# Expert 6's store in five parts on three DMA queues instead of three parts on two

## The chip, the cores and the metric

The kernel runs on one core of one Trainium2 chip. The metric is the device time of one execution in microseconds; a run is one such measurement, and the median of the runs counts. The profile is of one further execution: its span goes from the first to the last instruction that the hardware profiler recorded.

## The reference

Eight experts, each a layer of two products with biases and a ReLU between them, in fp32:

```python
n_experts, capacity, hidden, expert_hidden = 8, 256, 512, 2048
h = np.matmul(x, w1) + b1[:, np.newaxis, :]     # x (8,256,512), w1 (8,512,2048)
h = np.maximum(h, 0)
return (np.matmul(h, w2) + b2[:, np.newaxis, :]).astype(np.float32)   # w2 (8,2048,512)
```

w1 and w2 are 4 MB per expert each, so some 64 MB of weights are read, 4 MB of x, and 4 MB of results are written.

## The kernel before, in words

The experts are e = 0 to 7. All weights come from HBM as fp32 and are cast to fp16 on the way, by DMAs that GpSimd issues (`load_w1`, L84; `load_w2`, L93). Each weight tile is 128 partitions wide, and there are three tiles for w1 and three for w2, so a load waits until TensorE has finished with the tile's earlier contents. w2 of experts 6 and 7 comes in two halves (`HALVED`). x of experts 0 and 1 comes as fp32 through SyncE (L190) and is cast on VectorE; the other x come through GpSimd.

VectorE transposes x in blocks of 32x32 (`transposes`, L109 and L112). `first_product` (L121) makes 16 blocks of h, transposed, of 128x256 each, in PSUM; ScalarE adds the bias and applies ReLU (L128). `second_product` starts both halves of the 256 rows with b2 (a product with ones, L171) and adds the 16 blocks of h times w2 (L178). It runs LAG = 3 experts behind the first product. The GpSimd DMAs stand in an order that is written out by hand in `ring`, and `ordered` keeps program order for them and for the matmuls.

`store` copies the two PSUM halves to SBUF, one on VectorE (L156) and one on ScalarE (L157). The results of experts 0 to 3 and of 4 and 5 are gathered in two tiles (`GROUPS`), which `flush` writes through GpSimd's ring (L140): 2048 KB and 1024 KB, late in the program. The results of experts 6 and 7 are written by `store` itself as soon as the copies are done (L164). Each is a tile of 128 rows, one per partition, with 4 KB a row (two output rows of 512 fp32), 512 KB in all. Expert 7's tile goes out as one DMA by SyncE. Expert 6's is cut into parts by the table `PARTS`, whose entries are first row, row after the last, and whether ScalarE issues it:

```python
PARTS = {E - 2: ((0, 25, False), (25, 121, True), (121, 128, False))}
```

A DMA that SyncE or ScalarE issues goes through a hardware queue (q1 and q10 in the profile); one that GpSimd issues goes through a ring in memory (q0), in which its transfers follow each other.

The order at the end of the program is: GpSimd issues the last halves of w2, then the flush of experts 0 to 3, then that of 4 and 5. SyncE issues the first and third part of expert 6, then expert 7. ScalarE copies half of expert 6, issues its part, and copies half of expert 7. Then SyncE waits for all landings (L261).

Of the kernel before, what the change touches and what calls it, by code (L numbers as in the profile page):

```python
# [10 lines left out]
def kernel(  # L11
# [9 lines left out]
    nc = tc.nc  # L21
    fp32 = mybir.dt.float32
    fp16 = mybir.dt.float16
    E, T, H = x.shape
    M = w1.shape[2]
    P = 128
# [10 lines left out]
    HALVED = (E - 2, E - 1)  # L37


    PARTS = {E - 2: ((0, 25, False), (25, 121, True), (121, 128, False))}  # L40
    nXF32 = 2
    X_LOADS = {2: 2, 4: 4}

    def ordered(ins):
        return tc.keep_in_program_order(ins)
# [96 lines left out]
    def store(e, po):  # L142
        if e in group_of:
            first, n = group_of[e]
            split, rows = n, P // n
            if e == first:
                results[e] = group_pool.tile(
                    [P, split * nTB, H], fp32, tag=f"out{e}", name=f"out{e}")
        else:
            first, n, split, rows = e, 1, 1, P  # L150
            results[e] = out_pool.tile([P, nTB, H], fp32, tag="out", name="out")
        out_sb = results[first]
        at = (e - first) * rows
        for k in range(split):
            part = slice(k * rows, (k + 1) * rows)
            nc.vector.tensor_copy(out=out_sb[at : at + rows, k * nTB, :], in_=po[0][part])  # L156
            nc.scalar.copy(out=out_sb[at : at + rows, k * nTB + 1, :], in_=po[1][part])  # L157
        dst = out[first : first + n].rearrange("e (p r) h -> (e p) r h", r=split * nTB)
        if e in group_of:
            if e == first + n - 1:  # L160
                pending[first] = (dst, out_sb)
            return
        for p0, p1, scalar in PARTS.get(e, ((0, P, False),)):
            (nc.scalar if scalar else nc.sync).dma_start(out=dst[p0:p1], in_=out_sb[p0:p1])  # L164

    def second_product(e):
        po = []
        for tb in range(nTB):
            t = psum_o.tile([P, H], fp32, tag=f"po{tb}", name=f"po{tb}")
            po.append(t)  # L170
            ordered(nc.tensor.matmul(  # L171
                out=t, lhsT=ones1, rhs=b2_sb[0:1, e * H : (e + 1) * H], start=True, stop=False,
            ))
        half = nJ // 2 if e in HALVED else nJ
        for lo in range(0, nJ, half):
            for tb in range(nTB):
                for j in range(lo, lo + half):
                    ordered(nc.tensor.matmul(  # L178
                        out=po[tb],
                        lhsT=hT[e][:, j, tb * P : (tb + 1) * P],  # L180
                        rhs=w2_sb[e][:, j, :],
                        start=False,
                        stop=(j == nJ - 1),
                    ))
        store(e, po)

    x32 = []
    for e in range(nXF32):
# [4 lines left out]
        out=b2_sb,  # L193
        in_=b2.rearrange("e h -> (e h)").rearrange("(o f) -> o f", o=1),
# [12 lines left out]
    for b in range(nB):  # L207
        nc.vector.transpose(  # L208
            out=b1T[b * B : (b + 1) * B, nB - 1 - b : nB - 1 - b + nJ * B],
            in_=b1_rows.rearrange("r (i j) -> r j i", j=nJ),  # L210
# [55 lines left out]
```

## Time and profile before

| | us |
|---|---|
| median of 3 runs | 181.59 |
| lowest and highest run | 181.46, 181.81 |
| span of the profiled execution | 179.7 |
| median of the runs less that span | 1.9 |
| TensorE matmuls busy | 129.1 (72%) |
| VectorE busy | 88.0 (49%) |
| ScalarE busy | 70.2 (39%) |
| GpSimd busy | 13.1 (7%) |
| GpSimd's ring, packets, as a share of 16 DMA engines | 96.6% |
| last issue of a store (expert 7, by SyncE), from the span's start | 173.9 |
| from that issue to its landing | 4.8 |

The profiled execution has no time of its own beside the span. The runs are longer than the span by 1.9 us; the difference lies before the first and after the last recorded instruction.

How to read it: a core has 16 DMA engines, and the page gives their mean busy share in 40 slices. Packets are listed by queue, not by engine. Numbers of DMA landings are from issue to the last of a transfer's data. Times within the span are counted from its start.

### The profile page before, as it was taken

The page shows a single profiled execution, that of the slowest core. Times are in us where ns is not written, and L with a number is a line of the kernel's source. Part 1 is how long each engine was busy: PE and PEld are TensorE (multiplying, and loading weights), DVE is VectorE, ACT ScalarE, POOL GpSimd, SP SyncE. Part 2 cuts the span into 40 slices and gives each one's busy share as a digit, 9 for nine tenths or more (in the row PEclk, how much of TensorE's full clock was granted, in tenths as well). Part 3 has the DMA queues.
Part 4 walks back from the last instruction along what each step waited for, and adds up shares of the span by engine and source line. Part 5 has one row for each costly group of instructions (what it writes and reads, how often), then busy time and mean ns, then how long its engine had stood idle before and what let it go on. Part 6 is the DMA issues. An engine that isn't in the chain of part 4 may idle for free.

```text
span 179.7 us, 1958 instructions
## 1 busy us (share of the span) xinstructions
PE 129.1 (72%) x784; PEld 85.8 (48%) x784; DVE 88.0 (49%) x125; ACT 70.2 (39%) x151; POOL 13.1 (7%) x28
## 2 busy tenths in 40 slices
PE   0005099969595970899969597969497887999950
PEld 0004079969592320795369244844195332433420
DVE  0999942987000199999999998003200020301010
ACT  0000459969593022483099005950586020020010
POOL 7000002120201010001010001000200021010000
PEclk9999999999998798589999889999999996999996
DMA  5999999999999999999999999999999999999996
GB/s 216 251 226 199 233 212 197 233 224 193 228 230 192 221 233 215 197 230 230 204 208 230 219 193 233 226 193 222 230 215 197 233 206 204 223 212 215 335 420 250
DMA packets 3829, 40.56 MB, mean 226 GB/s; under 512 B 461, under 2 KB 477, under 8 KB 1133
## 3 DMA queue, kind: packets, MB, share of 16 engines
q0 software_dynamic: 3232, 38.35, 96.6%
q1 hardware_dynamic: 476, 1.70, 2.4%
q10 hardware_dynamic: 112, 0.39, 0.5%
q8 instruction: 6, 0.10, 0.2%
q14 instruction: 3, 0.02, 0.0%
HBM read 71.39 MB, written 4.19 MB: 421 GB/s over the span
## 4 chain that ended last, share of the span: by engine, by line
DMA 66%; PE 26%; POOL 2%; another core or an unknown queue 1%; issue 1%; ACT 0%; POOLq 0%
DMA w1sb<-in_w_dram 44%; DMA w2sb<-in_w_dram 22%; PE po L178 18%; PE ph L121 8%; PE po L171 1%; POOL w1sb L84 1%; ACT out L157 0%; POOL x L76 0%; POOL b_sb L192 0%; POOL b_rows L196 0%; POOLq L250 0%
## 5 line engine op out<-in xcount | busy, mean ns | idle before, releaser
L121 PE MATMUL ph<-xT,w1sb 128*128 128x256 f16 x512 | 63.6, 289 | 34.8 <-DMA w1sb<-in_w_dram 23.9
L121 PEld LDWEIGHTS <-w1sb 128*128 128x128 f16 x512 | 59.0, 147 | 40.3 <-DMA w1sb<-in_w_dram 32.6
L178 PE MATMUL po<-w2sb,hT 128*128 128x512 f16 x256 | 61.4, 402 | 9.4 <-DMA w2sb<-in_w_dram 9.4
L112 DVE STREAM_TRANSPOSE xT<-x 32x256 f16<-32x256 f16 (+1 forms) x64 | 53.1, 889 | 25.6 <-DMA x<-in_x_dram 18.7
L128 ACT ACTIVATE hT<-ph,b1T 128x256 f16<-128x256 f32 x128 | 56.2, 474 | 13.6 <-PE ph L121 13.4
L178 PEld LDWEIGHTS <-hT 128*128 128x128 f16 x256 | 25.9, 102 | 44.7 <-issue 19.3
L156 DVE COPY out<-po 32x512 f32<-32x512 f32 (+2 forms) x22 | 15.1, 688 | 54.0 <-PE po L178 53.8
L157 ACT COPY out<-po 32x512 f32<-32x512 f32 (+2 forms) x22 | 12.7, 579 | 69.7 <-PE po L178 69.5
L109 DVE STREAM_TRANSPOSE xT<-x 32x256 f16<-32x256 f16 x32 | 14.0, 436 | 0.5
L93 POOL DMA_DIRECT2D w2sb<-in_w_dram x10 | 5.3, 534 | 72.8 <-PE po L178 72.8
L128 ACT ACT_TABLE_LOAD x1 | 1.3, 1283 | 20.5 <-DVE b1T L208 20.5
L84 POOL DMA_DIRECT2D w1sb<-in_w_dram x8 | 4.5, 558 | 63.2 <-PE ph L121 62.4
L171 PE MATMUL po<-b_sb,ones 1*128 1x512 f16 x16 | 4.8, 379 | 0.0
L208 DVE STREAM_TRANSPOSE b1T<-b_rows 32x512 f32<-32x512 f32 x4 | 4.1, 1035 | 0.1
L201 DVE CAST x<-x 128x1024 f16<-128x1024 f32 x2 | 1.5, 757 | 3.3 <-DMA x<-in_x_dram 3.3
L140 POOL DMA_DIRECT2D out_dram<-out x2 | 1.1, 542 | 10.9 <-ACT out L157 10.9
L171 PEld LDWEIGHTS <-ones 1*128 1x128 f16 x16 | 0.9, 92 | 2.1 <-issue 2.1
L76 POOL DMA_DIRECT2D x<-in_x_dram x2 | 1.1, 552 | 0.0
L197 DVE MEMSET ones<- 1x128 f16 x1 | 0.2, 165 | 0.8 <-PEq L250 0.8
L196 POOL DMA_DIRECT2D b_rows<-in_b_dram x1 | 0.5, 515 | 0.0
L192 POOL DMA_DIRECT2D b_sb<-in_b_dram x1 | 0.5, 513 | 0.0
L250 POOL MEMSET const-float32-0.0<- 128x1 f32 x1 | 0.1, 99 | 0.2 <-issue 0.2
(3 smaller groups left out, 0.3 us busy)
## 6 DMA issues: line engine op xcount, KB each, us to landing
w1sb<-in_w_dram POOLq DMA_DIRECT2D x8, 2048.0 KB, 34.5
w2sb<-in_w_dram POOLq DMA_DIRECT2D x6, 2048.0 KB, 46.8
w2sb<-in_w_dram POOLq DMA_DIRECT2D x4, 1024.0 KB, 24.0
out_dram<-out POOLq DMA_DIRECT2D x1, 2048.0 KB, 26.8
x<-in_x_dram SPq DMA_DIRECT2D x2, 512.0 KB, 3.9
x<-in_x_dram POOLq DMA_DIRECT2D x1, 1024.0 KB, 30.8
out_dram<-out POOLq DMA_DIRECT2D x1, 1024.0 KB, 17.8
x<-in_x_dram POOLq DMA_DIRECT2D x1, 512.0 KB, 24.0
```

The source lines that it names most:

```text
L84: ordered(nc.gpsimd.dma_start(out=w1_sb[e], in_=w1[e].rearrange("(p kc) m -> p kc m", kc=nKC)))
L93: ordered(nc.gpsimd.dma_start(out=w2_sb[e][:, lo : lo + half], in_=src[:, lo : lo + half]))
L109: nc.vector.transpose(out=out[:, :, g, :, 0, :], in_=block[:, :, :, 0, :])
L112: nc.vector.transpose(out=out[:, tb, g], in_=block[:, tb])
L121: ordered(nc.tensor.matmul(out=ph, lhsT=w1_sb[e][:, kc, :].rearrange("p (q j) -> p q j", j=nJ)[:, :, j], rhs=xT[e][:, kc, :], start=(kc == 0),
L128: nc.scalar.activation(out=hT[e][:, j, :].rearrange("p (tb k i) -> p tb k i", tb=nTB, k=split), in_=ph.rearrange("p (tb i k) -> p tb k i", ...
L156: nc.vector.tensor_copy(out=out_sb[at : at + rows, k * nTB, :], in_=po[0][part])
L157: nc.scalar.copy(out=out_sb[at : at + rows, k * nTB + 1, :], in_=po[1][part])
L171: ordered(nc.tensor.matmul(out=t, lhsT=ones1, rhs=b2_sb[0:1, e * H : (e + 1) * H], start=True, stop=False,))
L178: ordered(nc.tensor.matmul(out=po[tb], lhsT=hT[e][:, j, tb * P : (tb + 1) * P], rhs=w2_sb[e][:, j, :], start=False, stop=(j == nJ - 1),))
L201: nc.vector.tensor_copy(out=t, in_=x32[e])
L208: nc.vector.transpose(out=b1T[b * B : (b + 1) * B, nB - 1 - b : nB - 1 - b + nJ * B], in_=b1_rows.rearrange("r (i j) -> r j i", j=nJ),)
```

## The change

Expert 6's 128 rows are stored in five parts. ScalarE issues 64 rows (it issued 96). SyncE issues 25 rows as before, though others, and 3 (it issued 7). GpSimd issues 11 and 25 rows into its ring, behind the two flushes, in descriptors of 2 KB, so two for each row. The sum is 128 rows as before. Nothing else in the program is different: the instructions of TensorE, VectorE and ScalarE stand in the same order, and GpSimd has two DMA instructions more, at its end.

```diff
-    PARTS = {E - 2: ((0, 25, False), (25, 121, True), (121, 128, False))}
+    PARTS = {E - 2: (
+        (0, 64, nc.scalar), (64, 89, nc.sync), (89, 100, nc.gpsimd),
+        (100, 125, nc.gpsimd), (125, 128, nc.sync),
+    )}
...
-        for p0, p1, scalar in PARTS.get(e, ((0, P, False),)):
-            (nc.scalar if scalar else nc.sync).dma_start(out=dst[p0:p1], in_=out_sb[p0:p1])
+        for p0, p1, queue in PARTS.get(e, ((0, P, nc.sync),)):
+            if queue is nc.gpsimd:
+                ordered(queue.dma_start(out=dst[p0:p1], in_=out_sb[p0:p1], max_dma_last_dim=2048))
+            else:
+                queue.dma_start(out=dst[p0:p1], in_=out_sb[p0:p1])
```

## The prediction, made before the changed kernel was run

> **What bounds the kernel now.** I began with the page: the slices, then the DMA queues.
>
> ```profile
> span 179.7 us, 1958 instructions
> DMA  5999999999999999999999999999999999999996
> GB/s 216 251 226 199 233 212 197 233 224 193 228 230 192 221 233 215 197 230 230 204 208 230 219 193 233 226 193 222 230 215 197 233 206 204 223 212 215 335 420 250
> ...
> q0 software_dynamic: 3232, 38.35, 96.6%
> q1 hardware_dynamic: 476, 1.70, 2.4%
> q10 hardware_dynamic: 112, 0.39, 0.5%
> q8 instruction: 6, 0.10, 0.2%
> ```
>
> The DMA engines are full in every slice but the first and the last. No compute engine is: PE has 72%. q0 is GpSimd's ring, q1 SyncE's queue, q10 ScalarE's. The six q8 packets are loads of instructions, and they matter below. Next the tail, in windows (core 0; PE, PEld, DVE, ACT, POOL, clock, DMA share, GB/s), and who waits at the end on SyncE.
>
> ```profile
> 166.40:173.90 7.50, 6.89 (x32) 2.94 (x30) 0.69 (x1) 0.57 (x1) 0.00 (x0) 1.00 0.99 377
> 173.90:177.00 3.10, 0.00 (x0) 0.00 (x0) 0.00 (x0) 0.02 (x1) 0.00 (x0) 0.95 0.97 404
> 177.00:178.50 1.50, 0.00 (x0) 0.00 (x0) 0.00 (x0) 0.00 (x0) 0.00 (x0) 0.50 0.63 257
> 178.50:179.70 1.20, 0.00 (x0) 0.00 (x0) 0.00 (x0) 0.00 (x0) 0.00 (x0) 0.50 0.00 0
> ```
>
> ```profile
> SPq L261 <- DMA out_dram<-out: 4.1, 3, 2.4
> ```
>
> All compute is over at 173.9. What follows is stores alone, at 404 GB/s, and then the share drops to 0.63 for 1.5 us: some of the sixteen engines are done and others are not. That part is the whole subject. The chain of waits ends in PE and a copy and does not show it, because the last stores have no instruction behind them:
>
> ```profile
> 166.28 7.03 PE po L178 x32
> 173.31 0.02 issue
> 173.33 0.59 ACT out L157
> ```
>
> The issues say what is in flight then: the two GpSimd flushes (2048 and 1024 KB, still landing at 175 and 177.5), expert 6's three parts, and expert 7's 512 KB.
>
> ```profile
> out_dram<-out POOLq DMA_DIRECT2D x1, 2048.0 KB, 26.8
> out_dram<-out POOLq DMA_DIRECT2D x1, 1024.0 KB, 17.8
> out_dram<-out SPq DMA_DIRECT2D x1, 512.0 KB, 4.8
> out_dram<-out ACTq DMA_DIRECT2D x1, 384.0 KB, 9.1
> ```
>
> **Sixteen ends.** The trace's DMA records give each packet's start, duration, size and queue, but no engine. From 166 us on each packet begins where one before it ended, so they can be chained into sixteen sequences; that is my own reconstruction. A packet of one 4 KB row lies 0.1555 us before the next. The closing 4-byte record of expert 7's store (8 rows on every engine) ends each sequence. Of expert 6's 128 rows:
> - five engines (group A) carry 12: 5 of SyncE's 25, 1 of its 7, 6 of ScalarE's 96. They end at 178.06, 178.25, 178.26, 178.40 and 178.41.
> - two (B) carry 7: 1 and 6. They end at 178.12 and 178.26.
> - nine carry 6, and fall in two sets: four (C) end at 178.29, 178.30, 178.32 and 178.425, five (D) at 177.04, 177.32, 177.37, 177.43 and 177.54.
>
> SyncE's queue has 60 closing records: 16 for each of its two loads and for expert 7, 5 for the 25 rows and 7 for the 7 rows. So 25 rows went to five engines and 7 rows to seven, the same five among them.
>
> Why B and C are late is shown by the closing records of the GpSimd loads: in sorted order they keep their distances from load to load, except that after each of the six instruction loads (36.5, 53.5, 83.9, 105.7, 134.8 and 159.6 us; 0.89 to 0.97 us each) one more sequence drops back by 1.07 to 1.13 us. Six sequences are hit once each, and they are B and C. The first two hit are the lowest two of the late set, which match B. So the instruction queue steps from one engine to the next, starting at B.
>
> **The change, part by part.** The bytes are unchanged, and so is everything up to 166.4 us. What changes is which engine carries which of the 128 rows.
> - ScalarE, 64 rows instead of 96: four on each engine instead of six. One issue of 0.38 us as before.
> - SyncE, 25 rows as before, five on each of A; 3 instead of 7, one on each of three of A. Issue 0.36 and up to 0.60 us, over by 167.4; expert 7's store behind them is issued at 173.94.
> - GpSimd, 11 and 25 rows: two more issues on POOL of 0.54 us each (the two flush rows: 1.1 us). They wait for the two copies of expert 6, done at 166.37; POOL has been free since 160.3, and behind them stands only the end of the program. The second also waits for the eighth-last earlier GpSimd transfer, a w2 load landed at 149.5: no wait. Both are over at about 167.6, and the ring still has flush data until 175.8 to 177.2, so this is hidden; it would cost its 1.1 us only if the ring ran dry.
> - Two transfers more on GpSimd's ring add two closing records on each engine. After a flush such a record takes 6 ns: 0.012 us.
> - Two descriptors of 2 KB for a row: the nearest row is the bias load, whose 4 KB packets (two rows of 2 KB) took 172 ns against 159 for one row. So 0 to 0.013 us a row. It could also be a gain if two were moved together better, which no row suggests.
> - SyncE waits for two more landings at the end. Its waits lie 0.06 us apart (177.56, 177.62, 177.69) and stand ahead of the last one, on expert 7, at 178.80. The GpSimd rows end before expert 7's last row on each engine, so nothing; without that cover 0.06 to 0.2 us.
>
> **Where GpSimd's rows land** is shown by no row: all its transfers in this trace run over sixteen engines. By SyncE's counts 11 rows take eleven engines, one each, and 25 take five, five each. Two rows of this trace speak on the place: SyncE always begins at the same engines, the instruction queue steps on. I take the second for a ring that GpSimd fills: 11 and 5 make 16, so the second transfer takes the five that the first left out. If the first starts at A, those five are D. Rows then, against before:
> - A: 4+5+1 and 1 from SyncE on three of them, 11 or 10 instead of 12. Latest end 178.41 - 0.16 = 178.26.
> - B: 4+1 = 5 instead of 7: 178.26 - 0.31 = 177.95.
> - C: 5 instead of 6: 178.425 - 0.156 = 178.27.
> - D: 4+5 = 9 instead of 6: 177.54 + 0.47 = 178.00, with the 2 KB price 178.07.
>
> The last is C at 178.27, plus 0.012 and up to 0.013: 178.29 against 178.425, so 0.14 us less. The profiled execution's span falls from 179.68 to 179.54. The median of the runs, 181.59, stands 1.91 us above the span; I leave that alone, and get 181.45. The most any sharing could bring: the mean of the sixteen ends is 177.99, 0.44 us before the last.
>
> The Trainium skill, "DMA: Bandwidth & Descriptors", section "Why a DMA increments its semaphore by 16 and not by 1", states the placing that I chose: a GpSimd transfer that doesn't use all sixteen takes consecutive engines from a round-robin cursor, with a count that divides the rows. It also names an exception in which the rows are spread over sixteen in equal lots; by that the sum would be the second rival's, +0.17. No run shows either yet. Its "Rules for kernel authors" speak against the change: spreading transfers over the issuing engines doesn't help, since all run on the same sixteen. By that rule alone the sum is 0; the sixteen ends, 1.39 us apart, show that the share of each engine is still worth something.
>
> **Rivals.**
> - *The 25 rows fall on full engines (slower).* If GpSimd, like SyncE, always starts at the same low engines, A gets 4+5+1+1+5 = 16 rows on three: 178.41 + 4 x 0.1555 = 179.04, +0.61, so 182.2. If it steps on but starts elsewhere, the five fall on A, B or C, three rows more than now on some of them: 0.30 to 0.47 later, 181.9 to 182.06. For it: SyncE's rows. Against it: the instruction queue's. It decides as soon as one engine of A or C gets more than one row above its rows of before.
> - *GpSimd spreads evenly (no measurable change).* 11 rows as one each on eleven, 25 as two each on twelve and one on a thirteenth. C gets 7 instead of 6 and A up to 13: +0.156 and 0.012, so 181.76. For it: every GpSimd transfer in the trace uses sixteen.
> - *More slack than one profile shows (faster).* If other executions have the late engines further behind, the two rows taken from B and one from C bring more, up to the 0.44: 181.15.
>
> **How the numbers follow.** A measurement here can tell about 0.2%, 0.36 us, so within 181.23 to 181.95 is no change. My forecast 0.60: 181.45, inside, with 0.15 of it below 181.23 because the three runs before spread from 181.46 to 181.81. Full engines 0.26: 181.9 to 182.2, mostly above 181.95 (0.24). Even spread 0.10: inside, 0.01 above. More slack 0.04: faster. Sums: faster 0.19, same 0.56, slower 0.25. The range runs from 181.2, near the best sharing, to 182.1, which takes in the full engines but for the lowest-start case.
>
> **What would show it.** Right: closing records of expert 7's store with the last near 178.28 and D within 0.3 us of it; q1 with 56 closing records (5 and 3 in place of 5 and 7); ten GpSimd packets of 2 KB, or five of 4 KB, on each of five engines that have no SyncE rows. Wrong: those packets on the engines with SyncE's five rows, or on those that dropped back; a last end after 178.5; or instruction loads that hit other engines than before.

## The result, and the profile after

The changed kernel takes 182.60 us (median of 6 runs, 182.05 to 182.75) against 181.59 (six runs, 181.46 to 181.81): 1.0044 times as long by the record's ratio of the runs, with a 95% interval of 1.0030 to 1.0057 (the two medians alone stand 1.0056 apart). The prediction was 181.45, with a range from 181.2 to 182.1. The profiled execution is one of the shorter ones, 182.08 us with a span of 180.3; its runs lie in two groups, near 182.06 and near 182.65.

The page of the changed kernel says the same as before on nearly everything:

```profile
span 180.3 us, 1961 instructions
DMA  5998998999999999999999999999999999999995
...
q0 software_dynamic: 3360, 38.50, 96.5%
q1 hardware_dynamic: 468, 1.69, 2.5%
q10 hardware_dynamic: 80, 0.26, 0.4%
q8 instruction: 6, 0.10, 0.2%
```

The rows have moved between the queues as the diff says, and the mean share of a queue does not show where they landed. The tail does. In the windows of the changed kernel (same columns as before) the two first stretches move nearly as many GB/s as before (375 against 377, 393 against 404), and the last one is no longer empty:

```profile
166.40:173.90 7.50, 5.48 (x25) 2.22 (x23) 0.69 (x1) 0.59 (x1) 0.00 (x0) 1.00 0.99 375
173.90:177.00 3.10, 0.00 (x0) 0.00 (x0) 0.00 (x0) 0.00 (x0) 0.00 (x0) 1.00 0.98 393
177.00:178.50 1.50, 0.00 (x0) 0.00 (x0) 0.00 (x0) 0.00 (x0) 0.00 (x0) 0.56 0.70 273
178.50:179.70 1.20, 0.00 (x0) 0.00 (x0) 0.00 (x0) 0.00 (x0) 0.00 (x0) 0.50 0.06 24
```

A share of 0.06 of sixteen engines for 1.2 us is 1.15 us of one engine: most have done, and a few work on. The DMA issues say which transfer waits for them. Expert 7's store, issued at 173.69 us (before: 173.94), lands 5.7 us after its issue instead of 4.8:

```profile
out_dram<-out SPq DMA_DIRECT2D x1, 512.0 KB, 5.7
...
out_dram<-out POOLq DMA_DIRECT2D x1, 100.0 KB, 12.5
out_dram<-out POOLq DMA_DIRECT2D x1, 44.0 KB, 12.7
```

Chained into sixteen sequences as for the prediction, the tail reads as follows. "Late" are the six engines that an instruction load (q8) has hit.

| engines | rows of expert 6 | of these late | end of expert 7's store |
|---|---|---|---|
| A, five, with SyncE's 25 rows | 10 or 11 | 0 | 178.11 to 178.41 |
| six others with one GpSimd row | 5 | 4 | 177.06 to 178.70 |
| five with five GpSimd rows | 9 | 2 | 178.05, 178.08, 178.09, and the two late ones 179.06, 179.11 |

The two last ends are late engines with five GpSimd rows each. Two further things stand in the records. Six of the 36 GpSimd rows took 321 to 749 ns instead of 159, and earlier on two of ScalarE's 64 took 211 and 444 ns. And a GpSimd transfer leaves a filler of 8 bytes on every engine that it does not use, one for each row of its share: 60 of them, 5 x 1 for the 11 rows and 11 x 5 for the 25. So the 25 rows lie on the five engines that the 11 left out, five each.

### The profile page after: what moved, and what is told of

Its sections match the earlier page's. It is cut to its first block, busy times and chain, and to the rows that moved or that the text cites. A ratio compares the mean times of both kernels' runs of the same rounds, so it can differ in the third digit from the quotient of the medians.

```text
span 180.3 us, 1961 instructions
## 1 busy us (share of the span) xinstructions
PE 129.9 (72%) x784; PEld 86.2 (48%) x784; DVE 87.8 (49%) x125; ACT 70.2 (39%) x151; POOL 14.9 (8%) x30
## 4 chain that ended last, share of the span: by engine, by line
DMA 58%; PE 21%; DVE 13%; issue 2%; ACT 1%; POOL 1%; DVEq 0%; ACTq 0%
DMA w2sb<-in_w_dram 39%; DMA x<-in_x_dram 19%; PE po L184 11%; PE ph L124 10%; DVE xT L112 6%; DVE xT L115 5%; DVE b1T L214 2%; DVE x L207 1%; ACT L131 1%; POOL w2sb L96 0%; ACT out L160 0%; PE po L177 0%; POOL w1sb L87 0%; ACT hT L131 0%; DVEq L115 0%
## 5 line engine op out<-in xcount | busy, mean ns | idle before, releaser
L87 POOL DMA_DIRECT2D w1sb<-in_w_dram x8 | 5.0, 621 | 62.8 <-PE ph L124 62.0
L168 POOL DMA_DIRECT2D out_dram<-out x2 | 1.3, 645 | 6.4 <-ACT out L160 6.4
L143 POOL DMA_DIRECT2D out_dram<-out x2 | 1.1, 542 | 7.7 <-ACT out L160 7.7
```

Of the source, the lines that this page charges most:

```text
L87: ordered(nc.gpsimd.dma_start(out=w1_sb[e], in_=w1[e].rearrange("(p kc) m -> p kc m", kc=nKC)))
```

## The experiments

Theory P: the time is set by which engines get GpSimd's five rows each, since late ones are among them; delays of single packets come on top. The rivals are in the expectations. Ratios are to the kernel before, on the same chip, with their 95% intervals; different experiments ran on different chips. Where a diff shows added lines alone, they take the place of the changed kernel's five parts. "The five" are the engines with five GpSimd rows each.

**A second and a third profile of the changed kernel** (no edit).

> The changed kernel once more, for a second profile: its six runs lie in two groups, 182.05 to 182.08 and 182.56 to 182.75. Theory P (placement): the 25 rows fall on five engines of which two are late ones (hit by an instruction load), in every run; so in the profile two of the five engines with five GpSimd rows finish the second flush 0.5 us or more after the other three, and the last end without delays is 178.86. The second group then has a longer delay of GpSimd packets on one of these two: a few packets of 300 to 750 ns more, +0.6 us. Rival I: the instruction loads hit other engines from run to run; then in the slower group three or more of the five are late and no packet is longer than in the first profile.

> The changed kernel a third time; two of the five were late in both earlier profiles (182.08 and 182.06), while its runs go up to 182.85. Theory E: four late in an execution of 182.5 or more, two in one near 182.1. Theory K: two in any case, and what is longer is delays of single packets.

Measured: e1_again 182.56 (182.06 to 182.85, 7 runs; ratio 1.0041, 1.0025 to 1.0056), profiled at 182.06; f3_again 182.19. In both two of the five are late, as in the first profile, and the last end is a late one of the five: 179.06 and 179.21. The rest of the spread is not seen in these profiles, because none of them is of an execution above 182.2.

**The 25 rows first** (the two GpSimd parts in the other order).

```diff
-        (0, 64, nc.scalar), (64, 89, nc.sync), (89, 100, nc.gpsimd),
-        (100, 125, nc.gpsimd), (125, 128, nc.sync),
+        (0, 64, nc.scalar), (64, 89, nc.sync), (100, 125, nc.gpsimd),
+        (89, 100, nc.gpsimd), (125, 128, nc.sync),
```

> GpSimd issues the 25 rows first and the 11 after them. It shows at which engine GpSimd's ring starts, since SyncE's 25 rows mark group A. Theory P with the start two engines ahead of A (14 of 16, if A is 0 to 4): three of the five engines with five GpSimd rows are in A and two are not; A's first three get 15 rows, 3 more than before, so the last end is near 178.87, 182.05 us. Rival I (the ring starts at A, and the instruction loads moved by two engines instead): all five are in A, 14 or 15 rows each, last end near 178.87 too. The times hardly differ, the overlap with SyncE's rows does: 3 of 5 or 5 of 5. Another start gives another overlap.

Measured: 182.39 (182.36 to 182.72; 1.0041, 1.0027 to 1.0055). All five engines with SyncE's 25 rows have GpSimd's 25 too, and they are the last five, 179.05 to 179.47. So GpSimd's ring starts at the same engine as SyncE, engine 0 of A, and steps on from there. That part of the prediction was right; what was not as it assumed is which engines the instruction loads hit.

**4 KB descriptors.**

```diff
-                ordered(queue.dma_start(out=dst[p0:p1], in_=out_sb[p0:p1], max_dma_last_dim=2048))
+                ordered(queue.dma_start(out=dst[p0:p1], in_=out_sb[p0:p1]))
```

> The same five parts, but with GpSimd's rows as one descriptor of 4 KB each. In the changed kernel six GpSimd packets took 321 to 749 ns instead of 159, and the last engine ended about 0.24 us later for it. Theory D (the pair of 2 KB descriptors is what delays): no GpSimd packet of 4 KB over 200 ns, last end near 178.86, 0.2 to 0.25 us less than the changed kernel, about 181.85. Theory Q (several engines read the same four partitions at once): the long packets stay, 182.1 or 182.6 as before. Theory S (a 4 KB descriptor is spread in equal lots over all sixteen engines): two rows on each of twelve engines, no engine with five, 181.6 to 181.8.

Measured: 181.94 (181.69 to 182.13, 11 runs; 1.0013, 1.0005 to 1.0022). Theory S holds for the sharing: the 25 rows lie two each on twelve engines and one on a thirteenth. The time is above the 181.6 to 181.8 that it gave. Theory D falls: GpSimd packets of 226 to 692 ns are there without 2 KB descriptors. The profile gives two places exactly: of the two engines that only the 25 rows reach, with two rows and with one, both are late; they are 11 and 12. The three that no GpSimd row reaches, 13 to 15, are early.

**Other rows, same counts** (the loop in `store` is changed too, so that it takes the slices).

```diff
-        (0, 64, nc.scalar), (64, 89, nc.sync), (89, 100, nc.gpsimd),
-        (100, 125, nc.gpsimd), (125, 128, nc.sync),
+        (slice(1, 128, 2), nc.scalar), (slice(0, 50, 2), nc.sync), (slice(50, 72, 2), nc.gpsimd),
+        (slice(72, 122, 2), nc.gpsimd), (slice(122, 128, 2), nc.sync),
```

> The same five parts and counts, on other rows: ScalarE stores the 64 odd rows, the others the even ones in order, so that GpSimd's 11 rows lie on 21 partitions instead of 11, two in each four partitions instead of four. Theory Q (several engines read the same four partitions at once): the packets of 671 to 749 ns fall to 320 or less, the last end falls to 178.86 to 178.95, 0.15 to 0.25 us less than the changed kernel, about 181.85. Theory D (2 KB descriptors): packets of 600 ns and more stay, 182.1 or 182.6.

Measured: 182.24 (181.83 to 182.88, 12 runs; 1.0030, 1.0017 to 1.0044). In its profile no packet of the tail takes longer than usual, two of the five are late, and the last ends are exactly these two, 178.76 and 178.80, where the expectation had 178.86 to 178.95. The profiled execution took 181.83, the shortest of its runs. So delays go away with every second row, as theory Q has it, but the runs spread as widely as before.

**Where the late engines are: a marker run, twice.**

```diff
+        (0, 64, nc.scalar), (64, 69, nc.sync), (69, 78, nc.sync), (78, 89, nc.sync),
+        (89, 101, nc.sync), (101, 114, nc.sync), (114, 128, nc.sync),
```

> A marker run: no GpSimd rows; ScalarE stores 64 rows (four per engine) and SyncE 5, 9, 11, 12, 13 and 14, one row on each of as many engines. The number of closing records of SyncE's queue on an engine then tells its place among the sixteen. The prediction took the six engines hit by an instruction load to be six neighbours, 5 to 10. Theory P: four of them are in 5 to 10 and two in 11 to 15, as the changed kernel's profile has it, so the hits are spread, not neighbours, and the same places are hit in each execution. Rival: the places change from execution to execution. Row counts are 10 on 0 to 4, 9 on 5 to 8, 8 on 9 and 10, 7, 6, 5 and 4 on the rest: late ones in 5 to 8 end three rows after the 6 of before, 178.9; about 182.0 us.

> The marker run once more, for a second execution's set of late engines. Theory P: the same places as in m1_marks. Rival: other places, but six again, each hit once. About 182.0 us.

Measured: 181.98 and 182.05. The records of m1_marks would not chain into sixteen sequences, so it tells nothing on the places. In m2_marks the late engines are two of 5 to 8, both of 9 and 10, and 11 and 12. With e3_wide that looked like 7 to 12: six neighbours, two further on than the prediction had them. But no row here tells 7 and 8 from 5 and 6. And without any GpSimd row behind the flushes, 13 of SyncE's rows in m1_marks took 199 to 628 ns, and two in m2_marks 199 and 300.

**No GpSimd rows.**

```diff
+        (0, 64, nc.scalar), (64, 89, nc.sync), (89, 125, nc.sync), (125, 128, nc.sync),
```

> GpSimd's rows taken away: ScalarE 64, SyncE 25, 36 and 3, so the ring holds nothing behind the flushes. 36 rows go over twelve engines, three each: A has 13 or 12 rows, 5 to 11 have 7, the rest 4. Theory P: the last end is a late engine of 5 to 10 with 7 rows or A's with 13, 0.16 us after that of before: 181.75, and no packet over 200 ns. Rival R (giving up ScalarE's 32 rows is what costs, not the place of GpSimd's): as slow as the changed kernel, 182.1 to 182.6.

Measured: 181.71 (181.46 to 182.17, 12 runs; 0.9992, 0.9967 to 1.0017). Giving up ScalarE's 32 rows costs nothing that can be told; rival R falls. The last end is A's with 12 rows, 178.57; the late ones with 7 rows end at 178.36 or before. One SyncE row, at 170.3, took 281 ns, against the expectation. The windows show an empty end again:

```profile
177.00:178.50 1.50, 0.00 (x0) 0.00 (x0) 0.00 (x0) 0.00 (x0) 0.00 (x0) 0.89 0.56 227
178.50:179.70 1.20, 0.00 (x0) 0.00 (x0) 0.00 (x0) 0.00 (x0) 0.00 (x0) 0.50 0.00 0
```

**The kernel before, twice more.**

> The kernel before, once more, for the place of its late engines. In its first profile both engines of group B (one row of SyncE's 7, places 5 and 6) were late; in the marker run the late ones are two of 5 to 8, then 9, 10, 11 and 12, and in the other kernels two of 11 to 15 are late, so 5 and 6 can't be. Theory E (the place goes with the execution): here the late six leave out B, or other engines are late than in the first profile. Theory K (it goes with the program): B is late again, with four of 7 to 15. 181.4 to 181.8 us.

> As b1_before, a third execution. Theory K: B late again. Theory E: another set. If an execution has the late set at 7 to 12, B ends a lag earlier, about 177.2, and the last end stays with four late engines of 6 rows, near 178.4: 181.5 to 181.8 us.

Measured: 181.34 and 181.55. Both engines of B are late in both, and with them four of 7 to 15; the last ends are A's, 178.35 and 178.55. It looked as if the place belonged to the program.

**The rows put where 7 to 12 late would want them.**

```diff
+        (0, 48, nc.scalar), (48, 61, nc.gpsimd), (61, 111, nc.gpsimd),
+        (111, 120, nc.gpsimd), (120, 127, nc.sync), (127, 128, nc.sync),
```

> Expert 6's rows placed by what the changed kernels showed (ring starts at engine 0, steps on; late engines 7 to 12): ScalarE 48 rows (three each), GpSimd 13 (one each on 0 to 12), 50 (five each on 13 to 15 and 0 to 6) and 9 (one each on 7 to 15), SyncE 7 and 1. Rows: 10 on 0 to 6 (11 on 0), 5 on 7 to 12, 9 on 13 to 15; the ring ends where it began. Theory P (the place of the rows sets the time): the late ones end one row earlier than before, 178.27, and without delays 181.45; with the delays of the changed kernel's profile up to 181.9. It is at least 0.3 us faster than the changed kernel though it stores twice as many rows by GpSimd. Rival R (rows by GpSimd cost as such): slower than the changed kernel, 182.6 or more. If the late engines are 5 to 10 here, 5 and 6 carry 10 rows and end 0.6 us late, 182.2.

Measured: 182.27 (182.06 to 182.92, 11 runs; 1.0032, 1.0021 to 1.0043). In its profile two of the late engines are among 0 to 6, which carry 10 rows; the other four are in 7 to 12. The fillers and SyncE's 7 rows give the classes. As neighbours the late six could only be 5 to 10 here, but nothing shows them to be neighbours. The two late ones with ten rows are the last to end, 178.65 and, with three delays, 179.12. The last sentence of the expectation came true as far as 5 and 6 go, and the kernel did not become the better version that it was meant to be.

**One and two instructions more.**

```diff
-        (100, 125, nc.gpsimd), (125, 128, nc.sync),
+        (100, 125, nc.gpsimd), (125, 127, nc.sync), (127, 128, nc.sync),                          # e7_even
+        (100, 125, nc.gpsimd), (125, 126, nc.sync), (126, 127, nc.sync), (127, 128, nc.sync),     # e8_odd
```

> The changed kernel with SyncE's last 3 rows as 2 and 1: one DMA instruction more, the same rows on each engine but one. In the kernels so far the profile counts 1958, 1958, 1958 and 1962 instructions where the late engines are 5 to 10, and 1959, 1961 (four times) and 1963 where two of them are in 11 to 15. Theory N (the place of the instruction loads goes with an even or odd number of instructions): 1962 here, late engines 5 to 10, GpSimd's five rows on 11 to 15 all early; last end 178.27 without delays, 181.4 to 181.6, at least 0.5 us faster than the changed kernel. Rival G (it goes with GpSimd's 36 rows or the number of its transfers): two of 11 to 15 late as before, 182.1 to 182.7.

> The changed kernel with SyncE's last 3 rows as three single rows: two DMA instructions more, 1963. Theory N: late engines 7 to 12 as in the changed kernel, last end 178.86 and later with delays, 182.1 to 182.7. Rival H (any further SyncE transfer moves the place, or helps otherwise): as e7_even, 181.4 to 181.6.

> e7_even with the rows of e4_evens (ScalarE the odd rows, the others the even ones), in whose profile no packet of the tail was delayed. Theory N with theory Q (delays come where several engines read the same four partitions): 1962 instructions, late engines 5 to 10, no packet over 200 ns, last end 178.27 to 178.3: 181.45, 0.1 to 0.2 us below the kernel before and below e7_even by what delays cost there. If delays have another cause, the same time as e7_even.

> The kernel before with SyncE's 7 rows as 6 and 1: 1959 instructions. Theory N: the late engines move to 7 to 12; engines 5 and 6 end a lag earlier, near 177.2, two of 11 to 15 end near 178.3 instead of 177.4. The last end stays with a late engine of 6 rows or with A, near 178.4, so 181.6, no difference. Rival G: late engines 5 to 10 as before, 181.6 too; only the profile tells them apart.

Measured: e7_even 182.32 (181.69 to 182.79; 1.0039, 1.0025 to 1.0053), e8_odd 182.57 (182.19 to 182.97; 1.0055, 1.0042 to 1.0067), e9_even_evens 182.07 (181.75 to 182.99; 1.0034, 1.0019 to 1.0050), e10_before_odd 181.56 (181.42 to 182.01; 1.0003, 0.9994 to 1.0012). Theory N falls: e7_even and e9_even_evens have the same 1962 instructions, and two and four of the five are late; e8_odd came to 1964 instead of 1963 and has four; e10_before_odd with 1959 keeps engine 5 late (it has one of SyncE's 6 rows but not the single one), where the theory had it early. With four late the end is longer. The last window of e9_even_evens, profiled at 182.78 and with no delayed packet among GpSimd's, beside the one above:

```profile
177.00:178.50 1.50, 0.00 (x0) 0.00 (x0) 0.00 (x0) 0.00 (x0) 0.00 (x0) 0.50 0.70 279
178.50:179.70 1.20, 0.00 (x0) 0.00 (x0) 0.00 (x0) 0.00 (x0) 0.00 (x0) 0.50 0.17 68
```

0.17 x 16 x 1.2 is 3.3 us of one engine: the four end at 179.17, 179.31, 179.32 and 179.55, all others by 178.57.

**Second profiles of two of these.**

> e8_odd once more. In its profile four of the five engines with five GpSimd rows were late, in the changed kernel's two, so the number of instructions (1964 there, 1962 in e7_even and e9_even_evens with two and four) does not decide it. Theory E (the place of the instruction loads differs from execution to execution of the same kernel): here another number than four of the five is late, and the time goes with it: none 181.5, two 182.1, four 182.6 and more. Theory K (fixed for a program): four again.

> e9_even_evens once more; four of the five were late in its profile (182.78), while its runs went from 181.75 to 182.99. Theory E: another number than four; none about 181.5, two about 181.8, four 182.7. Theory K: four again.

Measured: 181.93 and 182.07. Two of the five are late in each, where the same kernels had four at 182.74 and 182.78. The window of f2_even_evens:

```profile
178.50:179.70 1.20, 0.00 (x0) 0.00 (x0) 0.00 (x0) 0.00 (x0) 0.00 (x0) 0.50 0.05 20
```

So the instruction loads hit other engines in different executions of one kernel, and the time goes with it by 0.7 to 0.8 us. Theory K falls in its strict form. But the two profiles of each kernel are also from two chips, so the chip could be what differs. The spread of e9_even_evens on one chip, 181.75 to 182.99, speaks for the execution; b1_before and b2_before, two profiles of one kernel on one chip, have the same late classes. This stays open.

The six loads' own durations, which stand in every trace, say more about the places. In all nineteen profiles they follow one cyclic order of eight, to within 1 ns, and only the start differs:

| loads start at | profiles | durations of the six loads, ns | late among the five |
|---|---|---|---|
| the first of the eight | before, changed, and eleven more | 893, 893, 949, 945, 935, 974 | 2 (changed, f1_odd, f2_even_evens, f3_again) |
| the third | e9_even_evens | 949, 945, 935, 974, 975, 961 | 4 |
| the fifth | e2_swap, e8_odd | 936, 975, 974, 962, 893, 893 | 4 (e8_odd) |
| the seventh | e1_again, e4_evens, e7_even | 974, 961, 893, 893, 949, 945 | 2 |

The simplest reading is eight engines that take the loads in turn. The first two are then B, 5 and 6, which the first two loads hit in the kernel before. The next four are 9 to 12, of which m2_marks shows all four late and, in it and in e3_wide, 11 and 12. The last two lie among 13 to 15, since two of the five are late when the loads start at the seventh and four when they start at the third or fifth. By this reading the loads pass over 7 and 8, the late engines are not neighbours, and the kernel before, the changed one and e6_right had the same ones: 5, 6 and 9 to 12. It fits every profile whose ends can be read, but no run was made to test it: no row marks single engines from 7 to 15 in the kernel before. What sets the start is open.

## Why the prediction was wrong

- *DMA engines are what bounds the tail; bytes and issues don't matter.* Right. POOL's two issues took 1.28 us instead of 1.08 and were over at 166.4, and the waits at the end lay ahead of the last one, so both were hidden; e5_noring shows the shares without the ring at the time of before.
- *Where GpSimd's rows land.* Right in all of it: eleven engines and five (fillers), starting at A (e2_swap), the second transfer on the five left out. This is what the Trainium skill states in "DMA: Bandwidth & Descriptors", section "Why a DMA increments its semaphore by 16 and not by 1". Its exception, equal lots over sixteen, is what the 4 KB descriptors brought in e3_wide: in this kernel the 2 KB descriptors made the difference.
- *"If the first starts at A, those five are D".* This is the step that failed, and with it the sum's "D: 178.00". The second transfer did take 11 to 15, but D was only known as the five early engines among 7 to 15. That they are 11 to 15 came from "the instruction queue steps from one engine to the next", from 5 to 10, which no row showed. In the changed kernel's profiles two of 11 to 15 are late. By the reading of the loads' durations above, which no run tested, they were late in the kernel before too, as two of C, and D was 7, 8 and 13 to 15. With nine rows the two would end at 178.68 and 178.86 without delays, and the second of these is 0.44 us after the last end of before; C's 178.425 and three rows more make 178.89. The first rival's price for C was 0.30 to 0.47. So the slower rival, given 0.26, was the case.
- *2 KB rows at 0 to 0.013 us each.* Mis-sized. Six of 36 took 321 to 749 ns; on the two last engines 0.38 and 0.24 us. The sum of the profile is then 178.86 + 0.24 = 179.10 against 178.43: 0.68 us, and 0.6 in the span. It was not the descriptors' size: 4 KB ones are delayed as well. Nor was it GpSimd's ring alone, as SyncE's rows in m1_marks show. All eight profiles in which GpSimd stores neighbouring rows by 2 KB have delays of over 250 ns in GpSimd's rows, the three with every second row have none. Whether it is the SBUF side or the HBM side of the neighbouring rows was not separated.
- *The range.* It rested on one profile of each cause. The median of the runs lies 0.5 us above the profiled execution. Executions with four late engines among the five, such as those of e8_odd and e9_even_evens at 182.74 and 182.78, would account for it. That the changed kernel's own longer runs are such executions is an inference: its three profiles are of shorter ones.
- *The rule against the change*, from the Trainium skill's "DMA: Bandwidth & Descriptors", section "Rules for kernel authors", that spreading transfers over the issuing engines does not help, came nearer to the time with its sum of 0 than the prediction's 0.14 less. But it missed as well, and not by its reason: shares did move the ends, the wrong way.

## What to carry to other kernels

Where all DMA engines are full to the end, as here, the last engine's own queue sets the time, and a mean share hides it: chain the packets into engines and look at each end. Before giving an engine more because it was early in a profile, take several profiles and ask what made the others late; an even share, or more only for engines that were early in all of them (here 0 to 4), is what these profiles support; no run here came out faster than the kernel before beyond its interval. In the kernel before, those five carry the surplus, and no place seen for the six late engines touched them.

## What the runs showed that was not expected

- An instruction load of 16 KB takes 0.89 to 0.98 us of one DMA engine and puts it back by about 1.1 us for the rest of the program; six of them hit six different engines, and in another execution of the same kernel, on another chip, the six can be others (two or four of five given engines). Their durations repeat in one order of eight, with four different starts in nineteen profiles.
- A GpSimd transfer of 11 or 25 rows in 2 KB descriptors leaves 8-byte fillers on all engines that it does not use, 6 ns apart.
- A 4 KB row that usually takes 159 ns took up to 758 ns when several engines stored neighbouring rows through GpSimd's ring, and up to 628 ns through SyncE's queue (m1_marks). In the three profiles with every second row no row of the tail did.
